# A hybrid attention and state-space block on one core: TensorE's order written by hand for the S5 parameters, attention and the S5 scan

## The chip, the cores and the metric

The kernel runs on one core of one Trainium2 chip. The metric is the device time of one execution in microseconds; for the kernel before, three runs are known. The five engines of a core are called PE (TensorE, the matrix unit), DVE (VectorE), ACT (ScalarE), POOL (GpSimd) and SP (SyncE, which here only starts transfers). Each executes its own list of instructions strictly in order and waits for the others at semaphores.

## The reference

One layer is computed in float32 on 2048 tokens of 1024 features. Cut to what matters:

```
h = rmsnorm(x, norm1_g)
q, k, v, u, g_attn, g_ssm = split(h @ w_in)          # 512, 128, 128, 512, 1024, 1024 columns
A = windowed_gqa(q, k, v, sink)                      # 8 heads of 64, 2 KV heads, |i-j| <= 128
S = bidirectional_s5(u, lam, dt, B, C, D, w_glu)     # 32 groups of 16 channels, 64 complex states,
                                                     # a forward and a backward scan, then GELU and GLU
x = x + (sigmoid(g_attn)*(A @ w_attn_branch) + sigmoid(g_ssm)*(S @ w_ssm_branch)) @ w_out
x = x + (silu(rmsnorm(x) @ w_ffn_gate) * (rmsnorm(x) @ w_ffn_up)) @ w_ffn_down
y = rmsnorm(x, norm_f_g)
```

## The kernel before, in words

**Matmuls.** A float32 product is made of three passes of the faster fp32r type: each operand is split into a high part (a rounded copy, made by ACT or POOL: L383, L385; the flag `hi_on_act` chooses) and a low part (the rest, made by DVE: L386), and PE adds high x high, high x low and low x high (`PASSES`). `mm_t` (the matmul of L417) gives 128 output features x 512 tokens, for the S5 input `u`, the gates and the attention branch; `mm_tok` (L426) gives 128 tokens x 256 features, for K, V and Q. Names like `ps_pj<-h,w` in the profile are the PSUM tile that is written and the tiles that are read; `h` is the normed input of 1024 tokens ("a half"), `w` a column block of weights.

**Stages.** The work runs in three phases.

- Phase 1 does half 0 first: norm and transposes of x (L467), K and V, Q, `u`, then the tables of the S5 recurrence (`ssm_prep`), then attention with the rest around it. `ssm_prep` is a generator. DVE and POOL work out cosine, sine and power tables by outer products (`outer`, L207 to L209); these go to memory as `cD`, and the last ones are `E` and `F` (tile `ef`), four groups at a time in eight rounds. In each round PE transposes the four groups of `E` (L289, PSUM tag `nt`), and multiplies `F` by a padded matrix `bk` that POOL fills (L293, L296) to get the short convolution `T` (L300, PSUM tag `a`). `E`, `F` and `T` go to memory as `eD`, `fD`, `tD`. Between its steps the program issues the gates of half 0, columns 0 to 7, 24 matmuls to a column block of 512 tokens.
- Attention has 32 units: 16 blocks of 128 queries by 2 KV heads. A unit transposes Q (L562), forms four score tiles (L575), lets DVE find the maximum (L577) and ACT take the exponential (L578), has POOL scale by the reciprocal sum, transposes each of the two or three key blocks of the probabilities (L594), copies and splits those by ACT and DVE (L597, L598: high part, low part), and multiplies by V (L601, PSUM tag `c`). Between units stand the gates 8 to 15 of half 0 and the projections of half 1.
- Phase 2 runs the S5 scan, in 16 pairs of groups (`ssm_pair`). For a pair PE forms two state inputs X from `U` and `E` (L334, PSUM tags `a` and `b`); DVE multiplies them by cosine and sine (m, L339 to L342), POOL adds these to Y (L345, L346), DVE runs a forward and a backward scan (L356, L357), POOL and DVE turn the result back (n, L359 to L362; H, L364 and L365), and PE forms the output y of the pair from `T`, `U`, `F` and `H` (L368 to L370, PSUM tag `c`, two matmuls of 128x256 at each line; four steps of ACT and DVE make the GELU and write `yD`). Behind the pairs the program lists the gates of half 1 (16 column blocks) and the attention branch (`ps_pj<-at,w`; DVE splits its input at L386 and multiplies by the gate at L685).
- Phase 3 is the GLU (its input is read back from `yD`, L722 on POOL and L723 on DVE; `ps_pj<-y,w`), the state-space branch (`ps_pj<-S,w`), the output projection, and the feed-forward network.

**What sets the order.** The functions are called in the order above, but the order on every engine is chosen by the framework's scheduler, which simulates the program with a cost model and takes, on each engine, what it believes can go next by priority. So in the kernel before the gates of half 1 were already drawn forward into the attention stage and the scan. PSUM tiles rotate by tag (`pj`, `nt`, `a`, `b`, `c`), SBUF tiles by tag with a number of buffers.

Of the kernel before, what the change touches and what calls it, by code (L numbers as in the profile page):

```python
# [10 lines left out]
F32 = mybir.dt.float32  # L11
# [27 lines left out]
PASSES = ((0, 0), (0, 1), (1, 0))  # L39


def shape_tables():
# [18 lines left out]
            np.ascontiguousarray(cst, dtype=np.float32))  # L61

# [6 lines left out]
class Kern:  # L69
# [58 lines left out]
    def ssm_prep(self, pool, lam_re, lam_im, log_dt, b_re, b_im, c_re, c_im, d):  # L128
# [9 lines left out]
        def rows(src, nm):  # L138
            r = W([G, 2, ST])
            self.load(r, src.rearrange("d g p -> g d p"))  # L140
            ps = self.ps("nt", [128, G])
            pe.transpose(ps, r.rearrange("g d p -> g (d p)"), self.ident[:G, :G])
            t = one(nm, [128, G])
            v.tensor_copy(t, ps)
            return t

        lr, li = rows(lam_re, "lr"), rows(lam_im, "li")
# [4 lines left out]
        for i, src in enumerate((b_re, b_im)):  # L152
            for dd in range(2):
                self.load(B[64 * dd:64 * dd + 64, i], src[dd].rearrange("g p h -> p g h"))
        C = one("C", [128, 2, G, CH])
        for i, src in enumerate((c_re, c_im)):
            fl = src.rearrange("g h p -> (g h) p")
            for k in range(4):
                r = W([128, 2, ST])
                for dd in range(2):  # L160
                    self.load(r[:, dd], fl[128 * k:128 * k + 128, :])
                ps = self.ps("nt", [128, 128])
                pe.transpose(ps, r.rearrange("c d p -> c (d p)"), self.ident)
                s.activation(C[:, i].rearrange("q g h -> q (g h)")[:, 128 * k:128 * k + 128], ps, AF.Copy)
# [46 lines left out]
        with ExitStack() as es:  # L211
# [5 lines left out]
            for g in range(G):  # L217
# [4 lines left out]
                if g % 4 == 3:  # L222
                    yield
# [52 lines left out]
        for g0 in range(0, G, NG):  # L276
# [5 lines left out]
            Ff = F.rearrange("q g r t h -> q g r (t h)")  # L282
            self.store(self.fD[:, g0:g0 + NG], Ff)
            ET = W([128, NG, 2, 128])
            for hh in range(2):
                pt = self.ps("nt", [128, NG // 2, 2, 128])
                for i in range(NG // 2):
                    for r in range(2):
                        pe.transpose(pt[:, i, r], E[:, hh * NG // 2 + i, r].rearrange("q s h -> q (s h)"), self.ident)  # L289
                s.activation(ET[:, hh * NG // 2:(hh + 1) * NG // 2], pt, AF.Copy)  # L290
            self.store(self.eD[:, g0:g0 + NG], ET)
# [5 lines left out]
            pk = self.ps("a", [48, NG, 128])  # L297
            for i in range(NG):
                for r in range(2):
                    pe.matmul(pk[:, i], bk[:, r, i], Ff[:, i, r], start=(r == 0), stop=(r == 1))  # L300
            S = W([16, NG, 15 * CH])
            s.activation(S[:, :, 0:128], pk[32:48], AF.Copy)
            s.activation(S[:, :, 128:240], pk[0:16, :, 16:128], AF.Copy)
            mid = S[:, :, 112:128]
            u3 = pool.tile([16, NG, CH], F32, tag="u3", name="u3", bufs=1)
            v.tensor_tensor(u3, self.ident[:16, :16].unsqueeze(1).to_broadcast([16, NG, CH]),
                            dd_[:, g0:g0 + NG].unsqueeze(2).to_broadcast([16, NG, CH]), MULT)
            v.tensor_tensor(mid, mid, pk[0:16, :, 0:16], ADD)
            v.tensor_tensor(mid, mid, u3, ADD)
            for i in range(8):  # L310
                self.store(self.tD[16 * i:16 * i + 16, g0:g0 + NG], S[:, :, 16 * (7 - i):16 * (7 - i) + 128])
            if g0 + NG < G:
                yield
        es.close()
        yield


    def ssm_pair(self, pool, g0):
        nc, v, s, p, pe = self.nc, self.v, self.s, self.p, self.pe
        tl = lambda tag, sh, bufs: pool.tile(sh, F32, tag=tag, name=tag, bufs=bufs)  # L320
        E, F = tl("E", [128, 2, 2, 128], 2), tl("F", [128, 2, 2, 128], 2)
        T, U, cs = tl("T", [128, 2, 128], 2), tl("U", [128, 2, NC], 3), tl("cs", [128, 2, 2, NC], 2)
# [5 lines left out]
        self.load(F, self.fD[:, g0:g0 + 2])  # L328
        self.load(T, self.tD[:, g0:g0 + 2])
# [8 lines left out]
        m = [tl("m", sh, 4) for _ in range(4)]  # L338
# [5 lines left out]
        Y, W, a = tl("Y", sh2, 2), tl("W", sh2, 2), tl("A", sh2, 2)  # L344
# [13 lines left out]
        n = [tl("n", sh, 4) for _ in range(4)]  # L358
# [4 lines left out]
        H = [tl("H", sh, 2) for _ in range(2)]  # L363
        p.tensor_tensor(H[0], n[0], n[1], ADD)  # L364
        v.tensor_tensor(H[1], n[3], n[2], SUB)  # L365
        y = self.ps("c", sh)
# [44 lines left out]
    def mm_t(self, ps, W, H, kt, cs=slice(0, 128), sl=slice(0, 512)):  # L411

        n = 3 * kt
        i = 0
        for k in range(kt):
            for a, b in PASSES:
                self.pe.matmul(ps, W[a][:, k, cs], H[k][:, b, sl], start=(i == 0), stop=(i == n - 1))  # L417
                i += 1

    def mm_tok(self, ps, H, off, W, kt=8):  # L420
# [3 lines left out]
        for k in range(kt):  # L424
            for a, b in PASSES:
                self.pe.matmul(ps, H[k][:, a, off:off + 128], W[k // 4][b][:, k % 4, :], start=(i == 0), stop=(i == n - 1))  # L426
                i += 1

# [31 lines left out]
    def norm_t(self, src, tok, g, tags=("nt", "pj"), xs=None):  # L460

        xs = xs or self.norm_x(src, tok)
        H = [self.act.tile([128, 2, 512], F32R, tag="a", name="h") for _ in range(8)]
# [6 lines left out]
        return H  # L470
# [22 lines left out]
    def kv_proj(self, W, H, hh, t0):  # L493
        for t in range(t0, t0 + 4):
            ps = self.ps("pj", [128, 256])
            self.mm_tok(ps, H[t // 4], 128 * (t % 4), W)
            tk = hh * 8 + t
            kt = self.sm1.tile([128, NKV, 2, DH], F32, tag="kt", name="kt", bufs=2)
            self.rope_(kt, ps[:, 0:128].rearrange("p (n d) -> p n d", d=DH), tk, NKV, 2)
# [20 lines left out]
    def u_proj(self, w_in, H, hh):  # L520
        for j in range(4):
            W = self.w_cols(w_in, 6 + j)
            ut = self.act.tile([128, L, 128], F32, tag="a", name="ut")
            for q in range(2):
                ps = self.ps("pj")
                self.mm_t(ps, W, H[q], 8)
# [3 lines left out]
    def gates(self, w_in, H, hh, j0, j1):  # L530
        for jj in range(j0, j1, 2):
            js = range(jj, jj + 2)
            W = [self.w_cols(w_in, 10 + j) for j in js]
            o = [self.act.tile([128, HALF], F32, tag="a", name="go") for j in js]
            for q in range(2):
                for i, j in enumerate(js):
                    ps = self.ps("pj")
                    self.mm_t(ps, W[i], H[q], 8)
# [5 lines left out]
    def attn(self, pool, units):  # L544
        todo = []
        for b, n in units:
            todo.append(self.attn_front(pool, b, n))
            if len(todo) > 3:
                self.attn_back(pool, *todo.pop(0))
        for u in todo:  # L550
            self.attn_back(pool, *u)

    def attn_front(self, pool, b, n):
# [12 lines left out]
        v.scalar_tensor_tensor(Q[:, 1], qp, DH ** -0.5, Q[:, 0].bitcast(F32), MULT, SUB)  # L566
        st = self.sm1.tile([128, 5, 4], F32, tag="st", name="st", bufs=3)
        nm, sm, es, den = (st[:, i] for i in range(4))
        P = []
        for i in range(4):  # L570
# [8 lines left out]
            P.append(pt)  # L579
        v.tensor_tensor(es, self.sink[:, 4 * n:4 * n + 4], nm, ADD)  # L580
# [5 lines left out]
        return b, n, k0, k1, P  # L586

    def attn_back(self, pool, b, n, k0, k1, P):
        s, v, pe = self.s, self.v, self.pe
        o = self.ps("c")  # L590
        for kb in range(k1 - k0):
# [3 lines left out]
            pt = pool.tile([128, 2, 512], F32R, tag="pT", name="pT", bufs=3)  # L595
            tf = tp.rearrange("p i q -> p (i q)")
            s.activation(pt[:, 0], tf, AF.Copy)  # L597
# [567 lines left out]
```

## Time and profile before

| what | us |
|---|---|
| median of the runs (lowest, highest) | 2737.94 (2737.4, 2742.16) |
| the profiled execution's own time | 2731.56 |
| span of its trace | 2729.8 |
| PE busy | 2572.3 (94% of the span, 12090 matmuls) |
| DVE busy | 1905.8 (70%) |
| POOL busy | 1259.4 (46%) |
| ACT busy | 1026.0 (38%) |

In a busy row, "L417 PE MATMUL ps_pj<-h,w ... x228 | 61.9, 416 | 0.0" is a group of instructions: line, engine, operation, tile written and tiles read, the count, then the busy time in us and the mean of one in ns, then the engine's idle time just ahead of them with what released it. Matmuls overlap in PE's pipeline, so the mean of one (416 ns) is longer than the distance from one to the next; that distance is read from a run of many in the timeline. A timeline row gives the start, the duration of the run, engine, line and count, and in brackets the idle time before it with its releaser. A row of the stretch table gives the stretch, its length, busy time (and instructions) of PE, of its weight loads, of DVE, ACT and POOL, then PEclk, the clock that TensorE was granted as a share of full speed, then the DMA engines' share and GB/s.

In the trace phase 1 ends and the scan begins at about 795 us; the GLU's input arrives at about 1060 us.

### The profile page before, as it was taken

The page shows a single profiled execution, that of the slowest core. Times are in us where ns is not written, and L with a number is a line of the kernel's source. Part 1 is how long each engine was busy: PE and PEld are TensorE (multiplying, and loading weights), DVE is VectorE, ACT ScalarE, POOL GpSimd, SP SyncE. Part 2 cuts the span into 40 slices and gives each one's busy share as a digit, 9 for nine tenths or more (in the row PEclk, how much of TensorE's full clock was granted, in tenths as well). Part 3 has the DMA queues.
Part 4 walks back from the last instruction along what each step waited for, and adds up shares of the span by engine and source line. Part 5 has one row for each costly group of instructions (what it writes and reads, how often), then busy time and mean ns, then how long its engine had stood idle before and what let it go on. Part 6 is the DMA issues. An engine that isn't in the chain of part 4 may idle for free.

```text
span 2729.8 us, 34653 instructions
## 1 busy us (share of the span) xinstructions
PE 2572.3 (94%) x12090; PEld 2117.5 (78%) x12090; DVE 1905.8 (70%) x2734; ACT 1026.0 (38%) x1869; POOL 1259.4 (46%) x1016
## 2 busy tenths in 40 slices
PE   8996999999998886999979999998999999999998
PEld 7874788988886665887858878886888887877887
DVE  5798459544449996667557888877777777466567
ACT  4211258345432222344444444445444444111113
POOL 2486133111126662126116677655666654354226
PEclk9997999999998997999989999998999999999999
DMA  5344642333255655567575565657555557676557
GB/s 162 98 143 166 190 127 73 96 91 86 80 184 163 200 159 153 160 204 244 164 243 170 154 187 171 176 171 212 143 147 169 147 147 244 263 267 239 220 188 258
DMA packets 451918, 467.95 MB, mean 171 GB/s; under 512 B 82848, under 2 KB 381856, under 8 KB 446624
## 3 DMA queue, kind: packets, MB, share of 16 engines
q1 hardware_dynamic: 451744, 465.75, 54.2%
q8 instruction: 95, 1.56, 0.2%
q14 instruction: 79, 0.65, 0.1%
HBM read 299.99 MB, written 165.68 MB: 171 GB/s over the span
## 4 chain that ended last, share of the span: by engine, by line
PE 71%; DVE 12%; POOL 6%; DMA 6%; issue 3%; ACT 1%; SPq 0%; DVEq 0%; POOLq 0%; ACTq 0%
PE ps_pj L417 17%; PE ps_b L885 16%; PE ps_pj L885 10%; PE ps_a L885 10%; PE ps_pj L426 4%; PE ps_a L782 3%; PE ps_b L782 3%; DVE w L838 2%; PE ps_c L601 1%; PE ps_b L594 1%; DVE W L357 1%; DMA z<-z 1%; POOL wn L207 1%; DVE w L386 1%; PE ps_a L574 1%
## 5 line engine op out<-in xcount | busy, mean ns | idle before, releaser
L417 PE MATMUL ps_pj<-h,w 128*128 128x512 f32 x1920 | 484.8, 401 | 0.0
L417 PEld LDWEIGHTS ps_pj<-h,w 128*128 128x128 f32 x1920 | 356.6, 189 | 79.6 <-issue 2.8
L885 PE MATMUL ps_b<-H,w 128*128 128x512 f32 x1584 | 385.2, 392 | 7.8 <-DVE u L913 3.5
L885 PEld LDWEIGHTS ps_b<-H,w 128*128 128x128 f32 x1584 | 298.3, 189 | 73.5 <-DVE u L913 5.6
L885 PE MATMUL ps_pj<-H,w 128*128 128x512 f32 x1056 | 266.2, 396 | 18.4 <-ACT w L837 8.8
L885 PE MATMUL ps_a<-H,w 128*128 128x512 f32 x1056 | 256.3, 390 | 0.0
L838 DVE TENSOR_TENSOR w<-T,w 128x512 fp32r<-128x512 f32 x220 | 204.6, 934 | 72.0 <-ACT w L837 70.1
L885 PEld LDWEIGHTS ps_pj<-H,w 128*128 128x128 f32 x1056 | 201.1, 191 | 63.8 <-ACT c L898 9.9
L885 PEld LDWEIGHTS ps_a<-H,w 128*128 128x128 f32 x1056 | 198.9, 188 | 41.4
L838 DVE TENSOR_TENSOR w<-raw,w 128x512 fp32r<-128x512 f32 x165 | 196.4, 1192 | 49.0 <-ACT w L837 48.8
L386 DVE TENSOR_TENSOR w<-raw,w 128x1024 fp32r<-128x1024 f32 x111 | 152.7, 1376 | 102.2 <-ACT w L383 77.7
L837 ACT ACTIVATE w<-T 128x512 fp32r<-128x512 f32 x220 | 136.2, 626 | 223.0 <-PE ps_b L885 71.6
L885 PE MATMUL ps_b<-w,z 128*128 128x512 f32 x792 | 203.9, 392 | 5.9 <-DVE xa L1036 3.3
L585 POOL TENSOR_SCALAR P<-P,st 128x384 f32<-128x384 f32 (+1 forms) x128 | 73.9, 596 | 270.6 <-DVE st L583 127.7
L885 PEld LDWEIGHTS ps_b<-w,z 128*128 128x128 f32 x792 | 148.9, 189 | 40.0 <-DVE xa L1036 5.0
L856 POOL TENSOR_TENSOR T<-raw 128x512 f32<-128x512 f32 x55 | 84.6, 1538 | 155.6 <-DVE w L838 103.6
L426 PE MATMUL ps_pj<-w,h 128*128 128x256 f32 x1152 | 147.7, 283 | 2.1 <-DVE h L469 1.6
L837 ACT ACTIVATE w<-raw 128x512 fp32r<-128x512 f32 x165 | 103.0, 625 | 114.2 <-PE ps_pj L885 32.8
L885 PE MATMUL ps_a<-w,z 128*128 128x512 f32 x528 | 140.9, 392 | 3.4 <-DVE xa L1036 1.9
L1036 DVE TENSOR_TENSOR xa<-xa,ps_b 128x512 f32<-128x512 f32 x128 | 87.1, 684 | 81.5 <-PE ps_b L885 79.8
L426 PEld LDWEIGHTS ps_pj<-w,h 128*128 128x128 f32 x1152 | 140.3, 188 | 4.1 <-issue 1.8
L577 DVE CUSTOM_DVE_ANT_0 P<-ps_a,cst,nsink 128x384 f32<-128x384 f32 (+1 forms) x128 | 74.1, 596 | 97.9 <-PE ps_a L575 97.4
(320 smaller groups left out, 5105.7 us busy)
## 6 DMA issues: line engine op xcount, KB each, us to landing
z<-zs SPq DMA_DIRECT2D x308, 256.0 KB
z<-z SPq DMA_DIRECT2D x40, 1792.0 KB
raw<-in_w_in SPq DMA_DIRECT2D x52, 512.0 KB
raw<-in_w_ffn_gate SPq DMA_DIRECT2D x44, 512.0 KB
raw<-in_w_ffn_up SPq DMA_DIRECT2D x44, 512.0 KB
x<-in_x SPq DMA_DIRECT2D x32, 512.0 KB
gD<-go SPq DMA_DIRECT2D x32, 512.0 KB
tg<-gD SPq DMA_DIRECT2D x64, 256.0 KB
```

The costliest lines, as they stand in the source:

```text
L207: eng.tensor_tensor(m1, a0[0], a0[1], MULT)
L386: (lo_eng or self.v).tensor_tensor(lo, src, hi.bitcast(F32), SUB)
L417: self.pe.matmul(ps, W[a][:, k, cs], H[k][:, b, sl], start=(i == 0), stop=(i == n - 1))
L426: self.pe.matmul(ps, H[k][:, a, off:off + 128], W[k // 4][b][:, k % 4, :], start=(i == 0), stop=(i == n - 1))
L577: v.tensor_tensor_reduce(pt, sc, mk, -1.0, self.nsink[:, h:h + 1], ADD, ALU.min, nm[:, i:i + 1])
L585: p.tensor_scalar(P[i], P[i], den[:, i:i + 1], 1.0, MULT, MULT)
L782: self.pe.matmul(ps[t], M[k0 + k][:, a, 128 * t:128 * t + 128], W[b][:, k], start=(k0 + k + i == 0), stop=(k0 + k == 7 and i == 2))
L837: self.s.activation(hi, src, AF.Copy)
L838: self.v.tensor_tensor(lo, src, hi.bitcast(F32), SUB)
L856: eng.tensor_tensor(T[:, 0], b12, b11, SUB)
L885: self.pe.matmul(ps, a, b, start=(first and i == 0), stop=(i == n - 1), skip_group_check=True)
L1036: v.tensor_tensor(x[n], x[n], ps, ADD)
```

## The change

The order of PE alone is written by hand in three stages (`tc.manual_schedule(engines={PE})`); all other engines and all other stages keep the scheduler's order. Line numbers of the changed kernel: `mm_t` L450, `mm_tok` L460, split L413 to L416, transposes of E L326, `bk` product L332, scan X L360, y L398 to L400.

- Matmul helpers become generators (`mm_t_steps`, `mm_tok_steps`, `norm_t_steps`) that yield after three matmuls an estimate of their time; `run(gen, us)` issues so much of one.
- **S5 parameters**: the main chain is Q, `u` and gates 0 to 13 of half 0; each step of `ssm_prep` yields how much of the chain is to be issued behind it. The PE work of a round is moved to `ssm_turn`, in which the two halves of E's transposes go to PSUM tags `nt` and `c`. `hi_on_act` now holds for Q and `u` too.
- **Attention**: 32 units in a software pipeline over 35 steps, with fixed gaps (`FILL`, 1.3, 0.72 and 1.0 us to a gap in its three parts) that are filled from `half1` (gates 14 and 15, norm, K, V, Q and `u` of half 1, gates 0 to 2 of half 1). The transposes of K stand two tiles behind their matmuls (`k_turn`).
- **Scan**: gates 3 to 15 of half 1 are laid between the pairs, 15 us worth first and then twice 4.3 us per pair; y of a pair stands two pairs behind its X. The PSUM tile of y alternates between `c` and `nt`. The tiles m and n share one tag of 6 buffers (they had 4 each), A has 1 buffer (2), U 4 (3), H 4 (2); F and T are loaded behind H.

The core of the diff:

```
+def run(gen, us):
+    while us > 0:
+        c = next(gen, None)
+        if c is None:
+            break
+        us -= c
+    return us
...
     def ssm_turn(self, pool, g0, NG, E, F, bk, dd_):
...
+            pt = self.ps(("nt", "c")[hh], [128, NG // 2, 2, 128])
...
-        m = [tl("m", sh, 4) for _ in range(4)]
+        m = [tl("m", sh, 6) for _ in range(4)]
...
-        n = [tl("n", sh, 4) for _ in range(4)]
+        n = [tl("m", sh, 6) for _ in range(4)]
...
-        y = self.ps("c", sh)
+        yield
+        y = self.ps("nt" if g0 % 4 else "c", sh)
...
-            self.q_proj(w_in, H, 0, 0)
-            self.q_proj(w_in, H, 0, 1)
-            self.u_proj(w_in, H, 0)
...
-                for j in range(4):
-                    for _ in range(4):
-                        next(prep, None)
-                    self.gates(w_in, H, 0, 2 * j, 2 * j + 2)
+                main = chain(self.q_proj(w_in, H, 0, 0), self.q_proj(w_in, H, 0, 1), self.u_proj(w_in, H, 0),
+                             self.gates(w_in, H, 0, 0, 14))
+                with self.tc.manual_schedule(engines={mybir.EngineType.PE}):
+                    due = run(main, 4.0)
+                    self.hi_on_act = True
+                    for us in prep:
+                        due = run(main, due + us)
+                    rest(main)
...
+            def fill(i, k):
+                due[0] = run(f, due[0] + FILL[i // 16])
+
+            with self.tc.manual_schedule(engines={mybir.EngineType.PE}):
+                self.attn(ap, [(b, n) for b in range(16) for n in range(NKV)], fill)
+                rest(f)
...
-            for g in range(0, G, 2):
-                self.ssm_pair(pool, g)
-        self.gates(w_in, self.H1, 1, 0, 16)
+            gt = self.gates(w_in, self.H1, 1, G0, 16, 1, pool, bufs=2)
+            with self.tc.manual_schedule(engines={mybir.EngineType.PE}):
+                due = run(gt, 15.0)
+                P = [self.ssm_pair(pool, g) for g in range(0, G, 2)]
+                for i in range(len(P) + 2):
+                    if i < len(P):
+                        next(P[i])
+                    due = run(gt, due + 4.3)
+                    if i > 1:
+                        rest(P[i - 2])
+                    due = run(gt, due + 4.3)
+                rest(gt)
```

On PE where the S5 tables come in, before (`ef` is E or F, `cst` holds the identity):

```order
L417 MATMUL ps_pj<-h,w 128x512 x450
L289 MATMUL ps_nt<-cst,ef 128x128
L417 MATMUL ps_pj<-h,w 128x512 x2
L289 MATMUL ps_nt<-cst,ef 128x128 x3
L417 MATMUL ps_pj<-h,w 128x512 x10
L300 MATMUL ps_a<-ef,bk 48x128
L417 MATMUL ps_pj<-h,w 128x512 x2
L300 MATMUL ps_a<-ef,bk 48x128 x4
```

The same place now:

```order
L450 MATMUL ps_pj<-h,w 128x512 x501
L326 MATMUL ps_nt<-cst,ef 128x128 x4
L326 MATMUL ps_c<-cst,ef 128x128 x4
L332 MATMUL ps_a<-ef,bk 48x128 x8
L450 MATMUL ps_pj<-h,w 128x512 x39
L326 MATMUL ps_nt<-cst,ef 128x128 x4
L326 MATMUL ps_c<-cst,ef 128x128 x4
L332 MATMUL ps_a<-ef,bk 48x128 x8
L450 MATMUL ps_pj<-h,w 128x512 x36
```

51 more projection matmuls stand ahead of the first transpose; the first 16 matmuls of a round now stand together, and behind them 36 to 39 of the gates.

On PE in a middle stretch of the scan, before (`at` is the attention branch's input, not the gates'):

```order
L417 MATMUL ps_pj<-at,w 128x512 x18
L334 MATMUL ps_a<-U,E 128x256
L334 MATMUL ps_b<-U,E 128x256
L334 MATMUL ps_a<-U,E 128x256
L334 MATMUL ps_b<-U,E 128x256
L417 MATMUL ps_pj<-at,w 128x512 x12
L368 MATMUL ps_c<-U,T 128x256
L369 MATMUL ps_c<-H,F 128x256
L370 MATMUL ps_c<-H,F 128x256
```

And now:

```order
L450 MATMUL ps_pj<-h,w 128x512 x18
L360 MATMUL ps_a<-U,E 128x256 x2
L360 MATMUL ps_b<-U,E 128x256 x2
L450 MATMUL ps_pj<-h,w 128x512 x21
L398 MATMUL ps_nt<-U,T 128x256
L399 MATMUL ps_nt<-H,F 128x256
L400 MATMUL ps_nt<-H,F 128x256
```

What lies between the steps of a pair is now 36 to 39 matmuls of the gates, and the attention branch has left this stretch.

On PE at the end of the scan, before (`y` is the GLU's input, `S` its output):

```order
L368 MATMUL ps_c<-U,T 128x256
L369 MATMUL ps_c<-H,F 128x256
L370 MATMUL ps_c<-H,F 128x256
L417 MATMUL ps_pj<-y,w 128x512 x48
L417 MATMUL ps_pj<-S,w 128x512 x96
```

And now:

```order
L398 MATMUL ps_nt<-U,T 128x256
L399 MATMUL ps_nt<-H,F 128x256
L400 MATMUL ps_nt<-H,F 128x256
L450 MATMUL ps_pj<-at,w 128x512 x336
L450 MATMUL ps_pj<-y,w 128x512 x48
L450 MATMUL ps_pj<-S,w 128x512 x96
```

Before, the last two pairs' outputs stood directly ahead of the GLU's matmuls (`ps_pj<-y,w`); now 336 matmuls of the attention branch stand between them. In the changed kernel POOL's order in a pair is Y, n, H, and H of a pair stands ahead of Y of the next; before it stood behind it.

More of the change, by code (lines that the diff above doesn't have):

```diff
@@ L2 @@
 from contextlib import ExitStack
-from itertools import zip_longest
+from itertools import chain, zip_longest
 import numpy as np
@@ L61, in shape_tables, with mix @@
             np.ascontiguousarray(cst, dtype=np.float32))
+def run(gen, us):
[5 more added lines that the diff above has]
+    return us
+def mix(a, b, n):
+    for c in a:
+        yield c
+        for _ in range(n):
+            c = next(b, None)
+            if c:
+                yield c
+    yield from b
 def rest(gen):
@@ L136, in ssm_prep @@
         W = lambda sh: pool.tile(sh, F32, tag="w", name="w")
[L138 to L147, printed above, removed]
+        R = []
+        for src in (lam_re, lam_im):
+            R.append(W([G, 2, ST]))
+            self.load(R[-1], src.rearrange("d g p -> g d p"))
         dt = one("dt", [128, G])
@@ L154, in ssm_prep @@
                 self.load(B[64 * dd:64 * dd + 64, i], src[dd].rearrange("g p h -> p g h"))
+        yield 8.0
+        lr, li = (one(nm, [128, G]) for nm in ("lr", "li"))
+        for r, t in zip(R, (lr, li)):
+            ps = self.ps("nt", [128, G])
+            pe.transpose(ps, r.rearrange("g d p -> g (d p)"), self.ident[:G, :G])
+            v.tensor_copy(t, ps)
+            yield 1.5
         C = one("C", [128, 2, G, CH])
@@ L305, in ssm_prep @@
[L305 to L311, printed above, removed]
@@ L418, in mm_t, with mm_tok_steps @@
                 i += 1
[L420 removed]
+            yield 3 * 0.227
+    def mm_tok_steps(self, ps, H, off, W, kt=8):
         n = 3 * kt
@@ L460, in norm_t, with norm_t_steps @@
     def norm_t(self, src, tok, g, tags=("nt", "pj"), xs=None):
+        H = []
+        rest(self.norm_t_steps(H, src, tok, g, tags, xs))
+        return H
+    def norm_t_steps(self, H, src, tok, g, tags=("nt", "pj"), xs=None):
         xs = xs or self.norm_x(src, tok)
-        H = [self.act.tile([128, 2, 512], F32R, tag="a", name="h") for _ in range(8)]
+        H += [self.act.tile([128, 2, 512], F32R, tag="a", name="h") for _ in range(8)]
         for k in range(8):
@@ L541, in gates, with attn @@
                 self.store(self.gD[j][:, hh * HALF:(hh + 1) * HALF], o[i])
[L544 to L551, printed above, removed]
+    def attn(self, pool, units, fill):
+        A, B = {}, {}
+        for i in range(len(units) + 3):
+            fr = self.attn_front(pool, *units[i]) if i < len(units) else iter(())
+            sc = A.pop(i - 1, iter(()))
+            ba = self.attn_back(pool, *B.pop(i - 3)) if i - 3 in B else iter(())
+            next(fr, None)
+            next(ba, None)
+            fill(i, 0)
+            next(sc, None)
+            next(sc, None)
+            next(ba, None)
+            fill(i, 1)
+            next(sc, None)
+            next(ba, None)
+            fill(i, 2)
+            r = next(sc, None)
+            next(ba, None)
+            fill(i, 3)
+            rest(ba)
+            fill(i, 4)
+            if i < len(units):
+                A[i] = fr
+            if r:
+                B[i - 1] = r
     def attn_front(self, pool, b, n):
@@ new lines, in phase1, with half1 @@
+            due = [0.0]
+            def fill(i, k):
[3 more added lines that the diff above has]
+                rest(f)
+    def half1(self, x, g1, w_in, H):
+        xs = [self.act.tile([128, D], F32, tag="a", name="x") for _ in range(4)]
+        for t in range(4):
+            self.load(xs[t], x[1024 + 128 * t:1152 + 128 * t, :])
+        g = self.gates(w_in, H, 0, 14, 16, 2, self.raw, "raw")
+        for _ in range(16):
+            yield next(g)
+        H = self.H1
+        W = self.w_wide(w_in, NH * DH)
+        H.append([])
+        yield from mix(self.norm_t_steps(H[0], x, 1024, g1, ("nt", "pj"), self.norm_x(x, 1024, xs)), g, 2)
+        H.append([])
+        xs = self.norm_x(x, 1536)
+        kv = self.kv_proj(W, H, 1, 0)
+        for _ in range(16):
+            yield next(kv)
+        yield from mix(self.norm_t_steps(H[1], x, 1536, g1, ("nt", "pj"), xs), kv, 2)
+        yield from self.kv_proj(W, H, 1, 4)
+        yield from self.q_proj(w_in, H, 1, 0)
+        yield from self.q_proj(w_in, H, 1, 1)
+        yield from self.u_proj(w_in, H, 1)
+        yield from self.gates(w_in, H, 1, 0, G0)
```

167 lines of the change are left out of this document (97 added, 70 removed).

## The prediction

> **What bounds the kernel now.** I read the table of busy time by stretch first, since the change moves work between stages and PE is busy for 94% of the span.
>
> ```profile
> core 0: us, PE busy (x) PEld busy (x) DVE busy (x) ACT busy (x) POOL busy (x), PEclk, DMA share, GB/s
> 200.00:315.00 115.00, 84.06 (x422) 64.27 (x420) 89.63 (x150) 23.64 (x41) 55.12 (x49) 0.87 0.53 171
> 475.00:795.00 320.00, 320.00 (x1768) 275.88 (x1767) 148.78 (x384) 144.29 (x331) 47.56 (x84) 1.00 0.36 101
> 795.00:1076.00 281.00, 226.42 (x895) 175.25 (x894) 236.52 (x226) 61.45 (x97) 162.39 (x160) 0.92 0.56 171
> ```
>
> PE is the bound in the attention stretch (475 to 795: busy throughout at full clock). In two others it stands and its clock is lowered: the S5 tables (0.87) and the scan (0.92). "Busy" hides part of that, since a matmul at a lowered clock stays busy longer. So I count work by the distance between matmuls in dense runs.
>
> ```profile
> 95.60 105.16 PE L417 MATMUL ps_pj<-h,w 128*128 128x512 f32 x450
> 900.22 0.59 PE L368 MATMUL ps_c<-U,T 128*128 128x256 f32 x2
> 900.65 0.59 PE L369 MATMUL ps_c<-H,F 128*128 128x256 f32 x2
> ```
>
> 105.16/450 is 0.234 us for a 128x512 matmul; two 128x256 take 900.65 - 900.22 = 0.43, so 0.216 each. Then, by the groups of PE in the scan stretch (795.7 to 1076.2):
>
> ```profile
> L417 PE MATMUL ps_pj<-at,w 128*128 128x512 f32 x384 | 101.1, 413 | 14.2 <-DVE ma L685 10.7 <-DVE at L386 3.5
> L417 PE MATMUL ps_pj<-h,w 128*128 128x512 f32 x141 | 37.0, 412 | 0.0
> L368 PE MATMUL ps_c<-U,T 128*128 128x256 f32 x64 | 23.0, 445 | 19.1 <-issue 19.1
> L369 PE MATMUL ps_c<-H,F 128*128 128x256 f32 x64 | 22.3, 435 | 0.0
> L417 PE MATMUL ps_pj<-y,w 128*128 128x512 f32 x48 | 15.1, 479 | 12.0 <-POOL y L722 11.0 <-DVE y L723 0.6 <-ACT tz L732 0.3
> ```
>
> There are 573 matmuls of 128x512 (384 + 141 + 48), which at 0.229 to 0.234 are 131 to 134 us, and 320 of 128x256 (64 at each of five places: X to two PSUM tiles, and three for y), 69 us. That is 200 of work in 280.6 us, so 80.6 are lost. In the S5 stretch the same count:
>
> ```profile
> L417 PE MATMUL ps_pj<-h,w 128*128 128x512 f32 x228 | 61.9, 416 | 0.0
> L300 PE MATMUL ps_a<-ef,bk 128*48 128x128 f32 x128 | 19.5, 296 | 4.2 <-POOL bk L296 4.2
> L289 PE MATMUL ps_nt<-cst,ef 128*128 128x128 f32 x64 | 10.6, 287 | 26.8 <-DVE ef L209 26.8
> ```
>
> 228 x 0.234 = 53.3, and 192 of 128x128, a quarter of the width, at about 0.11 (estimated as half of the 0.216 for twice the width) = 21: 74 of work in 115 us, 41 lost. PE's instructions are the same in number in both kernels, 12090 matmuls. So the change can only move idle time and clock; it pays what it removes of 41 and 80.6, less any wait that it makes.
>
> **The S5 tables.** Before, PE ran out of projections and stood for the first E:
>
> ```profile
> 224.06 0.69 DVE L207 TENSOR_TENSOR wm<-ewr,B 128x512 f32<-128x512 f32 x1 [4.81 <-DMA cD<-wt]
> 227.54 0.45 PE L289 MATMUL ps_nt<-cst,ef 128*128 128x128 f32 x1 [26.78 <-DVE ef L209]
> 230.47 2.12 DVE L209 TENSOR_TENSOR ef<-wm 128x512 f32<-128x512 f32 x2
> 266.22 3.61 PE L300 MATMUL ps_a<-ef,bk 128*48 128x128 f32 x16 [4.15 <-POOL bk L296]
> ```
>
> Now 501 projections stand ahead, not 450, so PE comes to the first transpose at about 95.6 + 501 x 0.234 = 212.7. DVE's and POOL's chain to E is not shortened (the high split of Q's and u's weights goes from POOL to ACT, which is busy 23.64 of 115 there; I take nothing for it). E still comes at 227.5: 14.8 us of waiting are left. Behind it PE now stands for F too, since nothing lies between: the transposes end at about 228.5 and F at 230.47 + 2.12 = 232.6, 4 us. Then half clock: in the row of 266.22 sixteen matmuls took 3.61 where 16 x 0.11 is 1.8, so the 24 of this round lose some 2.3. POOL once took 20 us for two fills of `bk`:
>
> ```profile
> 245.97 20.20 POOL L296 TENSOR_SCALAR bk<-bb 64x128 f32<-64x128 f32 x2
> ```
>
> In its cover PE had gates to draw on and still stood 4.15 us and lost clock. With a fixed 36 gates (8.4 us) between rounds I take 6; the ends are 0 and 12 (20.2 less one gap of 8.4). With 1 us of hand-overs, 28 stay of 41: **13 saved**, between 0 (the fill starves twice) and 25 (E earlier by 10, as POOL has less to do). [...]
>
> **Attention.** The stretch has no idle time to win. What the fixed order may lose is the chain between the transposes of a key block and the product with V:
>
> ```profile
> L597 ACT ACTIVATE pT<-ps_b 128x512 fp32r<-128x512 f32 x41 | 24.0, 585 | 2.8 <-PE ps_b L594 2.8
> L598 DVE TENSOR_TENSOR pT<-ps_b,pT 128x512 fp32r<-128x512 f32 x41 | 28.1, 687 | 13.4 <-ACT pT L597 13.3
> ```
>
> ACT 0.585, then DVE 0.687, 1.27 us and some 0.15 of hand-over, and Q's copies ahead of them in part. In its place PE has a filled gap of 1.3 us (0.72 in the second half of the units) and two scores, four matmuls of 128x384 at three quarters of 0.234, 0.7: 1.4 to 2.0 us. It fits with nothing to spare: 0 to 0.15 us for each of 16 units, so 2 us, which K's delayed transposes may give back, and I put it at **0**; the ends are -6 and +25 (0.8 us a unit, when Q's copies hold both).
>
> **The scan.** Before, the attention branch stood between the pairs, and its DVE work (about 2.9 us a pair) between the scans:
>
> ```profile
> L685 DVE SCALAR_TENSOR_TENSOR ma<-tg,ps_pj 128x512 f32<-128x512 f32 x26 | 17.6, 679 | 0.2
> L386 DVE TENSOR_TENSOR at<-ar,at 128x512 fp32r<-128x512 f32 x12 | 17.0, 1454 | 0.0
> L357 DVE TENSOR_TENSOR_SCAN W<-A,Y 64x1023 f32<-64x1023 f32 x10 | 26.5, 2653 | 0.3
> L364 POOL TENSOR_TENSOR H<-n 128x512 f32<-128x512 f32 x9 | 19.5, 2164 | 0.2
> L360 POOL TENSOR_TENSOR n<-W,cs 128x512 f32<-128x512 f32 x10 | 17.0, 1700 | 0.0
> L345 POOL TENSOR_TENSOR Y<-m 128x512 f32<-128x512 f32 x9 | 11.5, 1273 | 2.5 <-DVE m L340 2.2
> ```
>
> (Groups of 880 to 1020, ten pairs; a split or so per pair is 1.45, and two `ma` 1.36.) That load leaves this stretch, and gates, whose weights cost DVE one split in most pairs, take its place. What sets the pace is a loop through DVE and POOL. One turn of it before:
>
> ```profile
> 908.67 2.27 DVE L356 TENSOR_TENSOR_SCAN W<-A,Y 64x1023 f32<-64x1023 f32 x1
> 913.34 1.28 POOL L359 TENSOR_TENSOR n<-W,cs 128x512 f32<-128x512 f32 x1 [6.75 <-DVE W L357]
> 914.58 1.75 POOL L360 TENSOR_TENSOR n<-W,cs 128x512 f32<-128x512 f32 x1
> 916.29 1.28 POOL L362 TENSOR_TENSOR n<-W,cs 128x512 f32<-128x512 f32 x1
> 917.54 1.28 POOL L345 TENSOR_TENSOR Y<-m 128x512 f32<-128x512 f32 x1
> 920.54 2.28 DVE L356 TENSOR_TENSOR_SCAN W<-A,Y 64x1023 f32<-64x1023 f32 x1 [1.78 <-POOL Y L347]
> 920.74 3.16 POOL L364 TENSOR_TENSOR H<-n 128x512 f32<-128x512 f32 x1
> ```
>
> From scan to scan it is 11.87 us. Over the 16 pairs the distance was 15.0, since some turns waited for DVE's other work or PE. POOL's H ran behind the next Y, beside the scans. Now H stands between n and Y, inside the loop: two scans 4.57, three n, H and two Y at 1.28 each 7.7, with hops and memsets 0.7: 13.0. At the means of the group rows (1.41, 1.70, 1.59 for n, 2.16 for H, 1.27 and 1.43 for Y, in sum 9.6) it is 14.9. The longer values belong to turns in which POOL runs beside DVE's scans, as 3.16 against 1.28 shows, and H now runs behind them; I take 14.0, nearer neither end.
>
> PE's own work for a pair is 20 x 0.216 + 36 to 39 x 0.234 = 13.0 us, so it hangs on the loop by 1 us a pair. From the first X to the last y: 6.3 until the first scan (X 0.9, four m at the 0.68 of L685, which has their shape, two Y, hops), 15 turns of 14.0, then the last pair's scans, n, H and y, 4.6 + 6.2 + 1.4: 228.5. PE has in it 126.6 of gates, 69 for X and y, and 48 matmuls of the attention branch (11): 206.6, so 22 are lost, in tails for the most part. Behind it stand 336 matmuls of the attention branch, 77 us:
>
> ```profile
> 852.07 1.19 PE L368 MATMUL ps_c<-U,T 128*128 128x256 f32 x2 [4.42 <-issue]
> 1060.38 1.22 PE L417 MATMUL ps_pj<-y,w 128*128 128x512 f32 x2 [11.05 <-POOL y L722]
> ```
>
> They cover the trip of y through memory and POOL's L722 (11.05 gone) and the half clock that came with it. About 2 stay at the GLU's own hand-over. So 24 of 80.6 stay: **56.6 saved**; at 13.0 a turn 15 more, at 15.0 a turn 15 less.
>
> The y two pairs late has H ready when PE gets there, if the pace is 14; its second PSUM tag keeps the GELU of one pair off the next. If a y waited as long in every pair as in the row of 852.07, the clock would follow: there, after a gap of 4.42, two matmuls take 1.19 instead of 0.59. Y's twelve at twice the time would cost 2.6 us a pair, 42 in all. [...] The rest has one answer: one buffer of A less, six shared m and n, U 4 and H 4 are read by engines that the loop spaces out, F and T are needed two pairs later; nothing is taken for them, and if A's build has to wait for the second scan, the 9 us of POOL until the next scan hide it.
>
> **The sum.** 13 + 0 + 56.6 = 69.6, and about 1 for K's transposes at the start. The profiled execution took 2731.56, so 2661; the runs' median stands 0.23% above it (2737.94), and 2661 x 1.0023 = **2667**.
>
> **The rivals.** *The loop stays at 15 or above* (chance 0.17): the mean of before was 15.0, and DVE's order is still the simulation's; a split of 1.45 in front of a scan would delay it. For this speaks that means above 1.28 occur in most POOL rows; against it that 2.9 us of DVE work go. Each 1 us is 15 us: 2682 at 15, 2697 at 16; with the lowered clock at y, which I give 0.03 of the 0.17, 2709. *The S5 stage gives nothing* (0.10): PE's fixed order cannot reach past a late `bk`, and the fill starves in more than one round, 12 us for each; 2680 with one such round more, 2695 with two. *Everything fits better* (0.13): POOL is free for E ten us sooner, and the loop runs at 13.0: 2667 - 10 - 15 = 2642. *It gets slower* (0.04): in attention, where PE is full, the copies of Q or a reciprocal come late, and PE, which before drew other matmuls forward, stands in every unit, and at gaps like the 4.42 above drops its clock. It must lose more than 70/32 = 2.2 us in each of 32 units to pass 2738; at 3 us it would be 2763. Against it speak 144.29 of 320 for ACT and 148.78 for DVE, half idle there. *The order is made by hand but waits only move* (0.02): what leaves PE's scan returns as an idle end, 2738.
>
> My forecast has the remaining 0.54, with its own 2650 to 2685. About 0.2% of the time, 5.5 us, is what a measurement can tell from no change. Faster: 0.54 + 0.17 + 0.10 + 0.13 = 0.94; same 0.02; slower 0.04. For eight in ten, the range runs from the better case with ten us more, 2632, to two unfavourable rivals at once, 2682 and 2695 less the forecast's 2667 each, 2710.
>
> **What would show it.** In the profile after, the first E transpose waits 10 to 20 us (26.78 before), and one or two rounds wait for `bk`; the attention stretch has PE idle below 10 us at full clock; scans follow each other every 13 to 15 us; the wait for L722 is gone; PE's mean clock rises from 0.978. I am wrong if attention shows idle PE in each unit, if the scans come at 16 us or more, or if the wait for E stays at 25.

## The result, and the profile after

| | before | changed kernel |
|---|---|---|
| median of 4 runs, us (lowest, highest) | 2739.27 (2737.4, 2742.16) | 2691.3 (2686.41, 2696.69) |
| ratio to before, 95% interval | | 0.9824 [0.9802, 0.9847] |
| profiled execution: span, us | 2729.8 | 2694.9 |
| mean granted clock | 0.978 | 0.978 |

The change gained 48 us, where 70 were forecast; the time lies in the range (2632 to 2710), 24 us above the forecast of 2667. The two profiled executions differ by 34.9 us, less than the medians: that of the changed kernel was its slowest run (2696.69), and that of the kernel before, at 2731.56, lay below all four of its runs here. The account below is made on these two.

By stretches (stretch, its length, PE busy, weight loads, DVE, ACT, POOL, then granted clock, DMA share, GB/s):

```profile
200.00:315.00 115.00, 97.98 (x488) 79.52 (x487) 88.49 (x149) 27.97 (x46) 57.66 (x44) 0.91 0.55 181
475.00:689.80 214.80, 210.98 (x1180) 178.48 (x1179) 143.20 (x377) 133.64 (x326) 53.76 (x96) 1.00 0.36 96
689.80:1042.40 352.60, 322.43 (x1333) 259.16 (x1331) 241.88 (x236) 79.66 (x125) 148.68 (x160) 0.95 0.54 165
```

The S5 stretch does 488 matmuls now, not 422. The attention stretch has 3.8 us in which PE stands. The scan starts at 689.8 instead of 795; its clock is 0.95 and PE stands 30.2 of its 352.6 us, so PE is still short of work there. PE's groups in the S5 stretch (200.5 to 315):

```profile
L450 PE MATMUL ps_pj<-h,w 128*128 128x512 f32 x312 | 75.4, 400 | 0.0
L332 PE MATMUL ps_a<-ef,bk 128*48 128x128 f32 x112 | 15.4, 296 | 2.5 <-DVE ef L234 2.5
L326 PE MATMUL ps_nt<-cst,ef 128*128 128x128 f32 x32 | 5.5, 294 | 14.5 <-DVE ef L234 14.5
L326 PE MATMUL ps_c<-cst,ef 128*128 128x128 f32 x30 | 5.0, 292 | 0.0
```

And in the scan (689.8 to 1042.4), the larger groups:

```profile
L450 PE MATMUL ps_pj<-h,w 128*128 128x512 f32 x557 | 147.1, 418 | 20.7 <-ACT go L588 20.7
L450 PE MATMUL ps_pj<-at,w 128*128 128x512 f32 x384 | 94.5, 406 | 6.4 <-ACT go L588 2.8 <-DVE at L416 2.1 <-DVE ma L794 1.6
L398 PE MATMUL ps_c<-U,T 128*128 128x256 f32 x32 | 11.3, 438 | 2.1 <-issue 2.1
L450 PE MATMUL ps_pj<-y,w 128*128 128x512 f32 x48 | 11.0, 390 | 0.0
```

The wait of the GLU's matmuls (`y,w`, 12.0 before) is gone. In its stead stands a releaser that had no row there before: `go`, ACT's tanh of the gates, which empties their two PSUM tiles. PE's row of one such wait, and what follows it at half clock (granted 0.50 from 891.4 to 893.9; two y matmuls in 1.05 us instead of 0.59):

```profile
891.37 1.65 PE L450 MATMUL ps_pj<-h,w 128*128 128x512 f32 x3 [5.80 <-ACT go L588]
892.82 1.05 PE L398 MATMUL ps_nt<-U,T 128*128 128x256 f32 x2
```

ACT at the same time:

```profile
875.88 0.58 ACT L588 ACTIVATE go<-ps_pj 128x512 f32<-128x512 f32 x1
887.63 1.33 ACT L376 ACTIVATE A<-edge,r 128x512 f32<-128x512 f32 x2 [11.17 <-DVE W L383]
888.88 0.57 ACT L402 ACTIVATE g<-ps_c 128x512 f32<-128x512 f32 x1
890.20 0.63 ACT L404 ACTIVATE g<-g 128x512 f32<-128x512 f32 x1 [0.75 <-DVE g L403]
890.74 0.58 ACT L588 ACTIVATE go<-ps_pj 128x512 f32<-128x512 f32 x1
```

ACT is not busy. It stands 11.17 us at A, the scan's factors, whose one buffer is free only when the second scan of the pair before ends (`W`, L383), and the next `go` is queued behind it. One turn of the loop from scan to scan, on DVE:

```profile
851.17 2.28 DVE L382 TENSOR_TENSOR_SCAN W<-A,Y 64x1023 f32<-64x1023 f32 x1 [1.67 <-POOL Y L373]
853.48 2.29 DVE L383 TENSOR_TENSOR_SCAN W<-A,Y 64x1023 f32<-64x1023 f32 x1
855.80 0.69 DVE L387 TENSOR_TENSOR m<-W,cs 128x512 f32<-128x512 f32 x1
857.71 0.69 DVE L403 SCALAR_TENSOR_TENSOR g<-g,ps_c 128x512 f32<-128x512 f32 x1 [1.22 <-ACT g L402]
859.10 0.69 DVE L405 SCALAR_TENSOR_TENSOR g<-g,ps_c 128x512 f32<-128x512 f32 x1 [0.70 <-ACT g L404]
860.18 1.74 DVE L391 TENSOR_TENSOR H<-m 128x512 f32<-128x512 f32 x1 [0.40 <-POOL m L388]
861.85 1.21 DVE L416 TENSOR_TENSOR w<-raw,w 128x1024 fp32r<-128x1024 f32 x1
862.98 0.68 DVE L365 TENSOR_TENSOR m<-ps_a,cs 128x512 f32<-128x512 f32 x1
863.58 0.68 DVE L366 TENSOR_TENSOR m<-ps_b,cs 128x512 f32<-128x512 f32 x1
867.14 2.28 DVE L382 TENSOR_TENSOR_SCAN W<-A,Y 64x1023 f32<-64x1023 f32 x1 [1.68 <-POOL Y L373]
```

(Two more m, at 864.18 and 864.78, are left out. The tile `m<-W,cs` is n, which shares m's buffers now.) This turn takes 15.97 us; over the fifteen turns of the sixteen pairs the mean is 15.5. DVE stands for 4.0 us of it: H, a weight split of the gates, and the next pair's four m all stand between two scans, and H takes 1.74 us where an m, or DVE's part of n, takes 0.68. POOL's half of H runs beside it, and POOL's Y can start only behind the second of the m:

```profile
855.85 1.80 POOL L385 TENSOR_TENSOR m<-W,cs 128x512 f32<-128x512 f32 x1 [4.56 <-DVE W L383]
860.11 1.26 POOL L390 TENSOR_TENSOR H<-m 128x512 f32<-128x512 f32 x1
864.41 1.30 POOL L371 TENSOR_TENSOR Y<-m 128x512 f32<-128x512 f32 x1 [2.85 <-DVE m L366]
```

### The profile page after: what moved, and what is told of

It is laid out like the page before. It is cut to its first block, busy times and chain, and to the rows that moved or that the text cites. A ratio compares the mean times of both kernels' runs of the same rounds, so it can differ in the third digit from the quotient of the medians.

```text
span 2694.9 us, 34635 instructions
## 1 busy us (share of the span) xinstructions
PE 2566.2 (95%) x12090; PEld 2124.8 (79%) x12090; DVE 1899.0 (70%) x2734; ACT 1033.9 (38%) x1878; POOL 1237.3 (46%) x1007
## 4 chain that ended last, share of the span: by engine, by line
PE 42%; DVE 5%; DMA 3%; POOL 2%; issue 2%; ACT 1%; POOLq 0%; DVEq 0%; ACTq 0%; SPq 0%
PE ps_b L1003 17%; PE ps_pj L1003 11%; PE ps_a L1003 11%; DVE w L956 2%; PE ps_a L900 1%; PE ps_pj L450 1%; PE ps_b L900 1%; DMA hr<-h 1%; DMA hr<-h1S 1%; DVE zs L956 1%; DMA z<-z 1%; DVE H L956 1%; ACT H L955 0%; DMA raw<-in_w_ffn_up 0%; POOL T L974 0%
## 5 line engine op out<-in xcount | busy, mean ns | idle before, releaser
L450 PE MATMUL ps_pj<-h,w 128*128 128x512 f32 x1920 | 491.7, 406 | 21.9 <-ACT go L588 21.9
L450 PEld LDWEIGHTS ps_pj<-h,w 128*128 128x128 f32 x1920 | 358.5, 190 | 104.9 <-ACT go L588 25.2
L416 DVE TENSOR_TENSOR w<-raw,w 128x1024 fp32r<-128x1024 f32 x111 | 149.8, 1350 | 72.4 <-ACT w L413 64.2
L413 ACT ACTIVATE w<-raw 128x1024 fp32r<-128x1024 f32 x93 | 98.0, 1055 | 158.5 <-PE ps_pj L450 84.8
L460 PE MATMUL ps_pj<-w,h 128*128 128x256 f32 x1152 | 154.0, 285 | 4.2 <-DVE h L509 1.8
L460 PEld LDWEIGHTS ps_pj<-w,h 128*128 128x128 f32 x1152 | 142.4, 189 | 7.9 <-issue 2.0
```

Source lines behind the costliest of these rows:

```text
L413: self.s.activation(hi, src, AF.Copy)
L416: (lo_eng or self.v).tensor_tensor(lo, src, hi.bitcast(F32), SUB)
```

## The experiments

Two theories could explain the missing gain in the scan. Theory **ACT**: holding ACT behind A is the cause, since the change took A's second buffer. Theory **loop**: the loop over DVE and POOL takes 15.5 us a pair whatever PE does, PE has 13.0 of work for it, and `go` is only where the slack shows. The first group ran on one chip with the changed kernel as its own measure; the later runs were made on other chips, so all are compared by their ratio to the kernel before, run beside each:

> The changed kernel itself, as the measure for the others of this group. Both theories: 2691 us or so, scans 15.6 us apart in the profile, about 25 us of PE waits for ACT's gate step (go, L588).

Measured: 2691.95 us, 0.9841 [0.9827, 0.9854] of before; scans 15.5 apart; 23.8 us of waits for `go`.

**A's second buffer.**

```
-        Y, W, a = tl("Y", sh2, 2), tl("W", sh2, 2), tl("A", sh2, 1)
+        Y, W, a = tl("Y", sh2, 1), tl("W", sh2, 2), tl("A", sh2, 2)
```

> A gets its second buffer back (Y has one instead of two, which the loop doesn't use). PE's order is the same. Theory ACT (ACT is held behind A's build, which waits for the scans; the gates' PSUM tiles behind it stay full and PE stands): PE's waits for go vanish, 25 to 33 us faster than the changed kernel. Theory loop (the DVE-POOL loop sets the pace at 15.6 us a pair, PE has only 13.0 of work for it, and the wait for go is only where its slack shows): the wait for go goes, a wait of the same size for H or X comes instead, scans stay 15.2 to 15.6 apart, 0 to 8 us faster.

Measured: 0.9833 [0.9818, 0.9848], the same as the changed kernel; scans 15.5 apart. PE's waits in the scan (waiting and awaited instruction, us in all, times, longest):

```profile
PE ps_pj L450 <- ACT go L588: 23.7, 8, 5.8
```

and ACT's:

```profile
ACT A L376 <- DVE W L383: 145.0, 14, 12.1
```

Neither theory's sign: the wait for `go` should have gone by both. The scheduler used the freed buffer to put A one pair earlier in ACT's list, where it waits for the same scan end as before. So this edit gave ACT nothing, and is no verdict on theory ACT.

**H behind the next Y.**

```
-        m = [tl("m", sh, 6) for _ in range(4)]
+        m = [tl("m", sh, 2) if k % 3 == 0 else tl("H", sh, 4) for k in range(4)]
+        self.mh = m[2:0:-1]
...
-        H = [tl("H", sh, 4) for _ in range(2)]
+        yield
+        H = self.mh if g0 + 2 < G else [tl("H", sh, 4) for _ in range(2)]
```

The list of work is split there, so that H of a pair comes behind Y of the next, into tiles that this Y has read; n gets four buffers of its own again.

> A keeps one buffer; H of a pair is made behind Y of the next on DVE and POOL (its tiles are those of two of the next pair's m), so that it leaves the loop from scan to scan. Theory loop: scans 13.5 to 14.5 apart, 17 to 30 us faster than the changed kernel. Theory ACT: ACT is held as before, 0 to 5 us faster.

Measured: 0.9825 [0.9812, 0.9839], 4 us by ratio below the changed kernel, inside both intervals; scans 15.1 apart. H left the chain, and the loop shortened by 0.4, not by 1 to 2. Both edits together:

> Both edits together. Theory loop: scans 12.9 to 13.8 apart, near PE's own 13.0, 28 to 40 us faster than the changed kernel. Theory ACT: as with A's second buffer alone, 25 to 33.

Measured: 0.9835 [0.9821, 0.9848]; scans 15.1 apart. Nothing more. The form of theory loop that I had, a chain of durations, falls short here. In the profile with H behind Y the first scan had grown:

```profile
846.18 3.37 DVE L384 TENSOR_TENSOR_SCAN W<-A,Y 64x1023 f32<-64x1023 f32 x1
849.58 2.29 DVE L385 TENSOR_TENSOR_SCAN W<-A,Y 64x1023 f32<-64x1023 f32 x1
```

and POOL at that moment:

```profile
846.11 1.30 POOL L393 TENSOR_TENSOR H<-n 128x512 f32<-128x512 f32 x1
```

The scan is longer by 1.08, nearly H's own 1.30. So a new form, theory **port**: some DVE and POOL instructions take turns, as this scan and H did, and where H stands hardly matters, since its time is added anyway. The name is a label: what the two would share is in no trace.

**POOL's half of H left out.** With H behind Y, two clears of its tile stand in its place.

```
-        p.tensor_tensor(H[0], n[0], n[1], ADD)
+        p.memset(H[0], 0.0)
+        p.memset(H[0], 0.0)
```

> H behind Y, and POOL's half of H left out: two clears of its tile, which read nothing, stand in its place for about as long. Theory port (DVE's instructions with two SBUF inputs and POOL's that read SBUF take turns, so a scan beside H takes 3.37 us instead of 2.28): the first scan comes down to 2.3 and the loop by 0.8 to 1.3 us a pair, 10 to 18 us faster than with H behind Y. Theory order (only the order of the chain counts, H is off it): scans stay 15.1 apart, within 4 us.

Measured: 0.9749 [0.9731, 0.9767], 21 us faster than with H behind Y (0.9825); scans 14.0 apart. That is a little more than the 10 to 18 told; the profiled executions differ by 16.5 us, which is what 15 turns shorter by 1.1 give. The groups of the first scan, with H on POOL (14 scans) and then with clears (13):

```profile
L384 DVE TENSOR_TENSOR_SCAN W<-A,Y 64x1023 f32<-64x1023 f32 x14 | 43.8, 3129 | 2.3 <-POOL Y L374 2.3
```

```profile
L384 DVE TENSOR_TENSOR_SCAN W<-A,Y 64x1023 f32<-64x1023 f32 x13 | 29.5, 2272 | 2.3 <-POOL Y L374 2.3
L393 POOL MEMSET H<- 128x512 f32 x12 | 6.4, 530 | 0.7
L394 POOL MEMSET H<- 128x512 f32 x12 | 6.4, 531 | 0.7
```

POOL was occupied beside the scan in both, for 1.30 us with H and for 1.06 with the clears, and the scan fell from 3.13 to 2.27 where POOL read no tile. Theory port holds for this scan and H, and order alone would have left 15.1. With the shorter loop and ACT's A as before, the waits for `go` fell from 22.4 to 12.2 us: they follow the loop.

**The stages undone, and a longer cover.** The second group leaves one stage at a time to the scheduler:

```
-                with self.tc.manual_schedule(engines={mybir.EngineType.PE}):
+                with ExitStack():
```

> The changed kernel with the S5 parameters and the projections beside them left to the scheduler again, the other two stages by hand. If the hand order carries this stage's gain (19 us less lost from 95 to 327 us than before), 13 to 20 us slower than the changed kernel. Rival: the gain came from the split of the high parts moved to ACT and from program order, 0 to 5 slower.

Measured: 0.987 [0.9854, 0.9886], 8 us slower than the changed kernel by ratio. PE stood 25.8 us for E instead of 14.3, so the order by hand carries a part of the gain: the size lies between the two expectations, and the interval just touches that of the changed kernel.

> Attention left to the scheduler, the other two by hand. If the hand order there pays nothing and costs nothing: within 5 us of the changed kernel. Rival: it sets which gates are left as cover for the scan; without it the scheduler draws gates of half 1 forward into it, and the scan has less between its pairs: 10 to 30 slower.

Measured: 0.9899 [0.9883, 0.9914], 16 us slower: the rival's size, and its mechanism in part. The loss lies at the passage from attention to the scan, where PE has no gates left to fill its waits:

```profile
689.74 2.04 PE L674 MATMUL ps_c<-pT,V 128*128 128x512 f32 x4 [5.20 <-DVE o L692]
697.59 6.88 PE L450 MATMUL ps_pj<-h,w 128*128 128x512 f32 x21 [5.81 <-ACT go L588]
```

The first scan starts at 709.8 instead of 697.3, which is 12.5 of the 16 us. Between the pairs PE lacks no more than before: the scans are 15.5 apart, and the waits for `go` there come to 22.3 us.

> The scan stage left to the scheduler, the other two by hand; buffers and program order as in the change. If the hand order carries the gain of the scan (24 us in the profiles): 15 to 35 us slower than the changed kernel, with scans still 15 to 16 us apart. Rival: program order, two PSUM banks for y and the attention branch listed behind carry it: 0 to 8 slower.

Measured: 0.9835 [0.9821, 0.9848], no difference. The scheduler, given the work in turns, made nearly the same order itself. So the listing had to be undone as well:

```
-                    due = run(gt, due + 4.3)
...
+            for g in range(0, G, 2):
+                rest(self.ssm_pair(pool, g))
+            rest(gt)
```

> The scan stage in the order of before (pairs one after another, y behind its own pair, gates of half 1 listed behind the pairs) and left to the scheduler, with the new buffers; the other two stages by hand. If listing the work in turns is what the scan gained by: 15 to 35 us slower than the changed kernel. Rival: the gain came from the attention stage leaving the gates over, and the scheduler fills the scan as well: 0 to 8 slower.

Measured: 0.9887 [0.9867, 0.9907], 13 us slower than the changed kernel, a little under the range; its turns were shorter (14.4), but PE stood at y again, 9.7 and 8.2 us at the two PSUM tiles and 13.8 for H. It is the listing of the work in turns, not the fixing of the order, that helped in the scan. The shorter turn shows what that listing costs: here DVE makes two of the next pair's m ahead of H, in gaps that it has, while with the work in turns all four come behind H.

```profile
845.90 0.68 DVE L365 TENSOR_TENSOR m<-ps_a,cs 128x512 f32<-128x512 f32 x1
846.50 0.68 DVE L366 TENSOR_TENSOR m<-ps_b,cs 128x512 f32<-128x512 f32 x1
849.67 1.77 DVE L391 TENSOR_TENSOR H<-m 128x512 f32<-128x512 f32 x1 [0.39 <-POOL m L388]
```

The cover ahead of E:

```
-            yield 8.5
+            yield 8.5 if g0 else 23.5
```

> 66 more matmuls of the gates ahead of the first transpose of E (15 us more of the chain), and so many fewer behind the last one. If PE's wait of 14.3 us for E is only a lack of cover: the wait goes to 0 to 2, the half clock behind it too, 14 to 20 us faster than the changed kernel. Rival: the gates' weight splits on DVE, drawn forward with them, push E back by as much as 4 us: 8 to 13 faster.

Measured: 0.9804 [0.9789, 0.9818], 10 us faster than the changed kernel (0.9841). The wait is gone, PE reaches the transposes when E is there:

```profile
214.80 14.63 PE L450 MATMUL ps_pj<-h,w 128*128 128x512 f32 x62
229.26 0.60 PE L326 MATMUL ps_nt<-cst,ef 128*128 128x128 f32 x4
```

It was lack of cover, as told. The size is the rival's, but not for its reason: DVE began E at 225.50 here and at 225.78 in the changed kernel, so nothing pushed E back. What is missing went to a new wait: with 66 matmuls fewer behind the last round, PE came earlier to the first transposes of Q in attention and stood 4.41 us for a load. The profile names that of x, which these transposes do not read; Q's own was issued beside it, at 322.60, and is the likelier one.

```profile
328.75 1.09 PE L630 MATMUL ps_b<-cst,q 128*128 128x128 f32 x4 [4.41 <-DMA x<-in_x]
```

**More work in the scan.** With that cover, the first two quarters of the attention branch go into the chain behind the gates, and the pieces grow:

```
-            gt = self.gates(w_in, self.H1, 1, G0, 16, 1, pool, bufs=2)
+            gt = chain(self.gates(w_in, self.H1, 1, G0, 16, 1, pool, bufs=2), branch_a())
...
-                    due = run(gt, due + 4.3)
+                    due = run(gt, due + 5.5)
```

> The longer cover ahead of E, and in the scan pieces of 5.5 us of matmuls instead of 4.3 twice a pair, with the first two quarters of the attention branch behind the gates in the same chain, so that PE has some 15.6 of work for a pair instead of 13.0. Theory loop (scan to scan takes 15.4 whatever PE does; PE's waits for go and its half clock are slack that other work can fill): the waits for go shrink below 8 us, 25 to 38 us faster than the kernel with the longer cover alone, scans 15.3 to 16. Rival: the attention branch's splits and products on DVE lengthen the loop as they did before: scans at 16.5 and above where they stand, 0 to 15 faster.

Measured: 0.972 [0.9702, 0.9738], 2659.05 us: 23 us faster than with the longer cover alone (25 to 38 were told), 33 faster than the changed kernel. The scans are 15.8 to 16.4 apart beside the gates and 16.8 to 20.2 beside the attention branch. The stretch with gates, then that with the branch:

```profile
690.00:860.00 170.00, 166.41 (x727) 136.32 (x726) 128.02 (x112) 45.82 (x73) 99.83 (x106) 1.00 0.53 167
860.00:925.00 65.00, 52.12 (x213) 41.47 (x212) 53.90 (x55) 10.70 (x19) 30.98 (x36) 0.89 0.53 163
```

and PE's waits from 660 to 1090 us:

```profile
PE ps_pj L451 <- DVE ma L795: 14.6, 4, 10.1
PE ps_pj L451 <- ACT go L589: 4.9, 6, 1.7
```

In the first stretch PE is the bound at full clock, with A's one buffer, and ACT held 8.5 us at each of eleven A (10.3 in the changed kernel); the waits for `go` are 4.9 us. That speaks against theory ACT: what was idle was slack. In the second, the rival shows: the products of the attention branch are emptied by DVE, in the loop, and PE stood once for 10.1 us.

> The kernel with the longer cover and the fuller scan, with H behind Y as well and pieces of 5.0 us instead of 5.5, so that PE has about 14.6 of work for a pair. Theory loop (the loop takes 15.1 with H behind Y, and PE's work fits into it): scans 15.1 to 15.6 apart instead of 16.4, 5 to 15 us faster than with pieces of 5.5. Rival: what the attention branch's tiles wait for on DVE decides the end of the stage, and the shorter turns only bring it on earlier: within 5 us.

The edit joins the two diffs above, with 5.0. Measured: 0.9722 [0.9709, 0.9735], the same. The first fourteen turns take 15.4 in the mean and the wait of 10.1 is gone, but the waits for `go` are back at 12.2 and the last turn takes 21.1. In that one DVE splits the branch's input for 3.6 us between two scans and PE waits for it, so the rival has the time right, and its mechanism shows in one turn. The kernel with fuller turns is the fastest here that computes all.

## Why the prediction was right or wrong

**The size of the S5 term.** By the prediction's own count, 312 x 0.234 + 174 x 0.11 is 92 us of work in 115, so 23 are lost and 18 saved, where 13 were forecast (0 to 25). The wait for E was 14.33 us (14.8 told), for F 2.5 (4 told). The fill of `bk` did run long once more, 15.0 us, but PE never stood for it; the 6 us taken for that were not lost. No trace here settles why such a fill takes 15 or 20 us.

**Attention.** At 3.8 us of idle PE it is within "below 10", and its 0 was nearly right as a stage. What I had not seen is that its order pays elsewhere: by the run without it 16 us, through the gates that it keeps for the scan's start.

**The step that failed: "I take 14.0".** The forecast had 24 us lost in the scan. Up to the matmuls on S there were 989 x 0.229 + 69 = 296 of work in 346.4 us (689.8 to 1036.15): 51 lost, so 30 saved instead of 56.6. The turn took 15.5 and not 14.0, 22.5 us over 15 turns; the rest, as I estimate, is the half clock behind waits of up to 5.8 us (granted 0.50 behind that one). The rival "the loop stays at 15 or above" gives 2689.5 for 15.5, between its 2682 and 2697, and 2691.3 came. That these lie so close is partly luck: 5 us more were saved in the tables, 13 went elsewhere (below), and the profiled execution stood 5.4 above the median where the forecast put it 0.23% below. Two things made the longer turn. I counted POOL's chain and let DVE's H, its split and the m run beside it, when all of these now stand between n and Y. And I put POOL at 1.28 each as if H only had to leave DVE's scans to be cheap: with H behind Y the first scan took 3.13 us in the mean, with the clears 2.27, and with H ahead of Y DVE's part of H takes 1.74 beside POOL's, where it took 0.68 with POOL idle in the kernel before (at 907.47). So the time that one of the two engines keeps the other waiting was added to the loop in both places. I had counted one side of it only, POOL's longer rows beside the scans, and not what POOL costs DVE. By sums from the rows, two scans 4.57, n and H on DVE 1.36 and POOL's six 7.7 are 13.6, and the two m between H and Y, which start 0.60 apart, make it 14.8; a split adds 1.21, to 16.0. The profile has three turns without a split, 14.8 each, and from the third turn on ten with one, 15.7 to 16.35. With two m ahead of H (the scan as listed before) the mean was 14.4. So their place goes with about 1.1 of the 1.5 that my 14.0 lacked, by an estimate from that run, in which PE's order differs too.

**The buffers of A.** "Nothing is taken for them" was argued badly: A's wait did not delay the loop, but it held the gates' tanh on the same engine, where PE then stood. The price of nothing may be right, as the run with fuller turns suggests, but it is not shown: whether A alone costs something could not be tried cleanly, since the second buffer did not free ACT.

**The tail.** The 11.05 us at L722 are gone, and the 77 us of the attention branch hide the trip of y, as told. That branch was also the cheapest work left to fill the turns: moving half of it cost none of this cover's effect, as 168 of its matmuls still stood behind the last y.

**The remainder.** 18 + 30 are 48 saved in the two stages; the profiled executions differ by 34.9. About 8 are lost between 315 and 690, as PE's idle time shows: 5.3 us from 315 to 475 (1.4 before) and the 3.8 of attention (0 before). The 1 us told for K's transposes at the start did not come either: PE stands 12.6 us in the first 95, and 12.4 before. About 5 come from the last phase (1658.8 us from the matmuls on S to the end, 1653.5 before), whose order the change leaves alone; in a second profiled execution of the same kernel it took 1653.0, so that part is one execution's own.

## What to carry to other kernels

When PE waits for other engines in a loop, find that loop's own time first, and add up the instructions that the trace shows taking turns (here a scan of 2.28 us took 3.37 beside POOL's H of 1.30), not only the longest engine's chain; here reordering moved the wait or shortened the loop by a little, while more independent work in each turn filled it. Here an idle ACT that stood 11.17 us at A held the `go` queued behind it, for which PE waited 5.80: a wait that names ACT can be a wait for DVE. Judge a hand-written order by undoing one stage at a time, since a stage with no idle time of its own may be the one that leaves work for the next.

## What the runs showed of the hardware that was not expected

A DVE scan of 64x1023 took 2.27 us beside POOL clears of 0.53 each and 3.37 beside a POOL addition of 1.30 that reads two tiles. In the changed kernel the DVE addition that makes H took 1.74 beside a POOL addition of 1.26 that had begun first. The DVE multiply of n took 0.69 where it began first, at 855.80, and POOL's n beside it took 1.80, where the next took 1.28: in these rows whichever came second waited. The m multiplies, which read PSUM and one tile, took 0.67 to 0.69 in the scans of all these runs, beside POOL too: the one at 864.78 took 0.68 within POOL's Y of 864.41, which took 1.30.

The clock of PE fell after shorter gaps than the one of 4.42 us that the prediction weighs. In the run with POOL's half of H left out, nine matmuls behind a gap of 2.29 us take 3.82 us, 0.42 each instead of 0.23. In the kernel before, nine behind a gap of 2.70 us (at 870.45) take 3.90, at a granted clock of 0.56. After the gap of 1.73 us in the run with fuller turns, 21 take 5.16, 0.25 each.

```profile
831.89 3.82 PE L454 MATMUL ps_pj<-h,w 128*128 128x512 f32 x9 [2.29 <-ACT go L592]
724.48 5.16 PE L451 MATMUL ps_pj<-h,w 128*128 128x512 f32 x21 [1.73 <-ACT go L589]
```
